# Strassen's block products in part of the first layer's up projection, and new matmul costs in the planner

## The chip, the cores and the metric

The kernel runs on one core of a Trainium2 chip. The time is device microseconds (us) of one execution. The profile was taken in one more execution of the same program; the views of its trace show what each engine did and what it waited for. PE multiplies matrices, DVE is the vector engine, ACT the scalar engine, POOL the GpSimd engine, SP issues most of the DMAs.

## The reference

Two layers work on 512 latent tokens and 256 context tokens of width 1024. Each layer has four head groups and then a gated feed-forward part; all numbers are float32. Only the latent tokens are an output, so the second layer's feed-forward part runs on 512 tokens, the first one's on all 768.

```python
D_FF = 2816
def conv_ffn(h, w_up, conv_w, w_down):
    up = h @ w_up
    a, b = up[..., :D_FF], up[..., D_FF:]
    return (jax.nn.silu(dwconv3(a, conv_w)) * b) @ w_down
...
def trunk_layer(x, xc, c, c_ctx, ang_r, ang_c, layer_idx, ctx_out,
...
    sh1, sc1, gt1, sh2, sc2, gt2 = [m[:, None, :] for m in adaln_params(c, w_ada, b_ada)]
...
    x = x + gt1 * (mix @ w_out)
    x = x + gt2 * conv_ffn(modulate(rmsnorm(x, g2), sh2, sc2), w_up, ffn_conv, w_down)
```

## The kernel before

Everything is kept transposed: features on the 128 partitions, tokens along the free dimension. A float32 product is made of three matmuls of a faster type: each operand is split into a high and a low part, and `passes` (L670) multiplies high by high, high by low and low by high. So every weight tile of 128x1024 (`wr`, one DMA of 512 KB) is cast by ACT (`wh`) and its rest subtracted by DVE or POOL (`wl`); this is `split_units` (L536), and `load_units` (L522) keeps the DMAs of a fixed list, `plan`, ahead of it.

The up projection of one layer has 44 output tiles: 22 feature tiles, each with a half a and a half b. One tile of the first layer is 8 blocks of the contraction x 3 passes x 2 groups of tokens (512 and 256): 48 matmuls (`proj_t`, L677). `up_a` (L1380) takes a tile of a from PSUM through the depthwise convolution (`conv3`: one ACT and four DVE instructions) and the silu; `up_b` (L1387) multiplies by b and splits the product, the hidden tile, into `hi` and `lo`.

The down projection goes by chunks of feature tiles, `FFN_CHUNKS` (L30), in both layers: after the up tiles of a chunk come the down products of the chunk before it, eight output tiles of 128x768. `add_parked` (L1320) scales each from PSUM by ACT (`ev`), and a DMA issued by POOL adds it to `xacc` in DRAM (`dma_add`, L191). The last chunk's products go with `x`, loaded back from `xacc`, into the next norm (`final_pass`, L1280).

While the first layer's feed-forward part runs, `next_ada` (L1351) computes modulation columns, 8 blocks for the first layer and 48 for the second, on DVE: for each a DMA of 512 KB into `adaw`, and one or two products of 1024 elements with a sum along them. It has the lowest priority of all strands. Its buffers take the place of five extra tiles of `S` (`NX`), which the second layer gets when it is done.

No instruction's place is written by hand. `Sched` (L76) is a planner that runs when the program is built: strands (generators) ask for instructions, each with a cost in us (`mms`, L207, for matmuls), and the strand whose instruction could start first gets its place; by the same times an instruction that several engines can do gets its engine. Each engine then runs its instructions in that order. Tiles in SBUF come from `Slots` (L324), 42 of 128x768 (`S`), 3 for raw weights (`WR`) and 5 for each part of a split (`WHI`, `WLO`); PSUM's eight banks come from `Banks` (L367).

## Time and profile before

| | us |
|---|---|
| median of 3 runs | 1537.25 (1537.16 to 1537.35) |
| the profiled execution: time | 1539.82 |
| the profiled execution: span, first to last instruction | 1537.9 |
| PE busy in the span | 1488.2 |
| DVE, ACT, POOL busy in the span | 912.2, 611.9, 246.3 |
| the first layer's feed-forward part, first up matmul to the end of its last products | about 356 to 901 |
| the second layer's attention and its projections | about 940 to 1134 |

The profiled execution took 2.57 us longer than the median, and its time is 1.9 us over its span. A matmul's end is modelled in the trace and matmuls overlap, so a matmul's length says less than the distance from one start to the next, or the count in a window.

### The profile page before, as it was taken

To read this page: it belongs to the slowest core of one execution; us is meant where nothing else is said; L and a number is where in the kernel's file an instruction comes from. 1 tells how busy PE (TensorE), PEld (TensorE's weight loads), DVE (VectorE), ACT (ScalarE), POOL (GpSimd) and SP (SyncE) were. 2 spreads that over 40 slices of the span, in tenths; PEclk is the share of its full clock that TensorE was granted. 3 is DMA by queue.
4 is the path that set the end of the run, shared out by engine and by line. 5 is a ranking of instruction groups with operands and counts; after the bars stand their busy time and mean duration, and the time that the engine had idled before them with its cause. 6 is when DMAs were issued, how large, how long until landed. Compare 5 with 4: busy or idle time off the path is not lost.

```text
span 1537.9 us, 22293 instructions
## 1 busy us (share of the span) xinstructions
PE 1488.2 (97%) x8880; PEld 1259.5 (82%) x8880; DVE 912.2 (59%) x1475; ACT 611.9 (40%) x921; POOL 246.3 (16%) x263
## 2 busy tenths in 40 slices
PE   6999999999999999999999999989989999999997
PEld 4887777887888888888888879867779888888887
DVE  4757888657774746535445277778876443434335
ACT  4445455224333232332322343645534433333332
POOL 0201412013001010010100233144131011010111
PEclk9999999999999999999999999999999999999998
DMA  9573713114437384483763834242322456273644
GB/s 375 167 219 124 218 44 116 59 49 149 164 125 191 123 196 147 140 203 131 178 169 113 181 121 151 88 118 86 111 87 96 125 143 144 96 159 98 143 101 129
DMA packets 70184, 214.36 MB, mean 139 GB/s; under 512 B 9888, under 2 KB 12064, under 8 KB 69952
## 3 DMA queue, kind: packets, MB, share of 16 engines
q1 hardware_dynamic: 49920, 160.39, 32.2%
q0 software_dynamic: 18720, 51.10, 16.0%
q8 instruction: 70, 1.15, 0.3%
q10 hardware_dynamic: 1440, 1.44, 0.3%
q14 instruction: 34, 0.28, 0.1%
HBM read 165.70 MB, written 35.65 MB: 131 GB/s over the span
## 4 chain that ended last, share of the span: by engine, by line
PE 83%; DVE 6%; issue 6%; DMA 4%; ACT 1%; POOL 1%; SPq 0%; DVEq 0%; ACTq 0%; POOLq 0%
PE banks L211 81%; PE banks L224 2%; DVE ss L263 2%; DMA adaw<-in_w_ada 2%; DMA stk<-rlo 1%; POOL xacc L193 1%; DVE p L277 1%; DVE x L277 0%; DVE mx L303 0%; DMA x<-xacc 0%; DVE out L277 0%; DVE hlo L277 0%; DMA mats<-in_mats 0%; SPq L184 0%; ACT wh L253 0%
## 5 line engine op out<-in xcount | busy, mean ns | idle before, releaser
L211 PE MATMUL banks<-hhi,wh 128*128 128x512 f32 (+1 forms) x1392 | 427.6, 358 | 2.6 <-ACT hhi L243 2.4
L211 PE MATMUL banks<-hlo,wh 128*128 128x512 f32 (+1 forms) x1392 | 421.8, 353 | 0.8 <-DVE hlo L277 0.8
L211 PE MATMUL banks<-hhi,wl 128*128 128x512 f32 (+1 forms) x1392 | 420.3, 352 | 0.0
L263 DVE TENSOR_TENSOR wl<-wr,wh 128x1024 fp32r<-128x1024 f32 (+1 forms) x155 | 191.2, 1237 | 177.8 <-ACT wh L253 175.8
L211 PEld LDWEIGHTS banks<-hhi,wh 128*128 128x128 f32 x1392 | 233.8, 190 | 48.2 <-issue 10.2
L211 PEld LDWEIGHTS banks<-hhi,wl 128*128 128x128 f32 x1392 | 234.1, 190 | 38.9
L211 PEld LDWEIGHTS banks<-hlo,wh 128*128 128x128 f32 x1392 | 234.6, 190 | 36.8 <-DVE hlo L277 1.6
L253 ACT CAST wh<-wr 128x1024 fp32r<-128x1024 f32 (+1 forms) x188 | 195.8, 1044 | 149.0 <-PE banks L211 144.2
L193 POOL DMA_DIRECT2D xacc<-ev x80 | 69.2, 865 | 783.7 <-ACT ev L290 710.2
L211 PE MATMUL banks<-hi,wh 128*128 128x512 f32 (+1 forms) x560 | 170.5, 346 | 0.9 <-DVE x L277 0.9
L211 PE MATMUL banks<-lo,wh 128*128 128x512 f32 (+1 forms) x560 | 170.1, 346 | 0.0
L211 PE MATMUL banks<-hi,wl 128*128 128x512 f32 (+1 forms) x560 | 169.5, 344 | 0.0
L277 DVE SCALAR_TENSOR_TENSOR fy<-banks,vec,fy 128x511 f32<-128x511 f32 (+1 forms) x132 | 86.1, 659 | 133.3 <-ACT fy L243 131.4
L290 ACT ACTIVATE ev<-banks,ada 128x512 f32<-128x512 f32 x120 | 69.6, 614 | 148.6 <-PE banks L211 148.4
L265 POOL TENSOR_TENSOR wl<-wr,wh 128x1024 fp32r<-128x1024 f32 (+1 forms) x33 | 80.1, 2428 | 278.8 <-ACT wh L253 247.4
L243 ACT ACTIVATE fy<-banks,vec 128x768 f32<-128x768 f32 (+1 forms) x44 | 34.9, 795 | 215.0 <-PE banks L211 215.0
L211 PEld LDWEIGHTS banks<-hi,wh 128*128 128x128 f32 x560 | 95.0, 188 | 15.3 <-DVE x L277 1.3
L211 PEld LDWEIGHTS banks<-hi,wl 128*128 128x128 f32 x560 | 95.4, 188 | 14.5
L211 PEld LDWEIGHTS banks<-lo,wh 128*128 128x128 f32 x560 | 95.5, 188 | 13.3
L263 DVE TENSOR_TENSOR fy<-banks,fy 128x768 f32<-128x768 f32 (+1 forms) x44 | 36.3, 824 | 92.5 <-PE banks L211 92.4
L277 DVE SCALAR_TENSOR_TENSOR adaw<-adaw,silu 128x1024 f32<-128x1024 f32 x56 | 68.4, 1222 | 28.7 <-DMA adaw<-in_w_adaT 27.8
L303 DVE TENSOR_REDUCE mx<-banks 128x1 f32<-128x768 f32 (+1 forms) x80 | 67.8, 847 | 20.2 <-PE banks L211 19.2
(184 smaller groups left out, 2025.1 us busy)
## 6 DMA issues: line engine op xcount, KB each, us to landing
wr<-in_w_up SPq DMA_DIRECT2D x88, 512.0 KB, 3.7
adaw<-in_w_adaT SPq DMA_DIRECT2D x56, 512.0 KB, 4.5
wr<-in_w_dn SPq DMA_DIRECT2D x44, 512.0 KB, 3.4
adaw<-in_w_ada SPq DMA_DIRECT2D x40, 384.0 KB, 6.1
xacc<-ev POOLq DMA_DIRECT2D x40, 384.0 KB, 6.3
wr<-in_w_zt SPq DMA_DIRECT2D x24, 512.0 KB, 4.5
xacc<-ev POOLq DMA_DIRECT2D x40, 256.0 KB, 4.8
wr<-in_w_o SPq DMA_DIRECT2D x16, 512.0 KB, 3.3
```

The lines of the kernel that those rows point to most:

```text
L193: yield from self.op([("pool", 1.05, lambda: self.nc.gpsimd.dma_start(out, in_, accum_op=ALU.add))], [], [in_])
L211: self.nc.tensor.matmul(o, l, r, start=a, stop=b)
L224: self.nc.tensor.transpose(o, i, ident)
L243: return ("act", cost, lambda: self.nc.scalar.activation(out, in_, func, **k), func), outs, ins
L253: opts.append(("act", 0.19 + n / 1200, lambda: self.nc.scalar.copy(out, in_)))
L263: opts.append(("dve", 0.09 + n / 960, lambda: self.nc.vector.tensor_tensor(out, a, b, op=op)))
L265: opts.append(("pool", 0.1 + n * 2.25e-3, lambda: self.nc.gpsimd.tensor_tensor(out, a, b, op=op)))
L277: lambda: self.nc.vector.scalar_tensor_tensor(out, a, s, b, op0=op0, op1=op1, **k))], outs, ins)
L290: emit = dict(act=lambda: self.nc.scalar.activation(out, a, AF.Copy, scale=s), dve=lambda: self.nc.vector.tensor_scalar(out, a, s, None, o ...
L303: lambda: self.nc.vector.tensor_reduce(out, in_, axis=AX.X, op=op), [out], [in_])
```

## The change

The first layer's up projection has 4 plain feature tiles, as before, and 18 in nine pairs by Strassen's scheme in Winograd's form. A pair has a "quad" for a and one for b. A quad cuts the product of 256 features x 1024 inputs x 768 tokens into 2 x 2 x 2 blocks and makes seven block products in place of eight, each of 4 blocks of the contraction x 3 passes on 384 columns: 84 matmuls in place of 96. The operands' sums are made ahead: those of the weights in `split_quad`, by DVE on the raw tiles, so a quad has 3.5 tiles of 1024 to split where two plain tiles have 2; those of the input once, in `right_factors`. The products' sums are made from PSUM (`half_sums`, `quad_a`, `quad_c`), in four banks of which three are used twice: the products p2, p3 and p4 add to a bank that an engine has read before.

The chunks of the down projection become pairs in both layers (nine of 2 and one of 4, in place of 2, 4, 4, 4, 4, 4), so there are nine additions to `xacc` for each output tile in place of five: 64 more DMAs. There are 44 tiles in `S` and 4 for raw weights; the ring for the descriptors of POOL's DMAs is smaller. The planner takes 0.000449 us for a column of a matmul and 0.004 us with it, in place of 1/2400 and 0.003, and a lower least cost, 0.06.

```diff
-FFN_CHUNKS = [2, 4, 4, 4, 4, 4]
+FFN_CHUNKS = [2] * 9 + [4]
...
-NS = 42
+NS = 44
...
         for o, l, r, a, b in items:
-            c = max(0.107, self.n(r) / 2400 + 0.003)
+            c = max(0.06, self.n(r) * 0.000449 + 0.004)
...
+                for i in range(0, nf, 2):
+                    if quads(l, f):
+                        for c, o in (("a", 0), ("b", 1)):
+                            plan.append((f"q{c}{l}.{f}", [a["w_up"][l, 2 * f + o], a["w_up"][l, 2 * f + 2 + o]], 1024))
+                        f += 2
+                        continue
...
+        def split_quad(key):
...
+            yield from K.when(lambda: len(raws) >= 2)
+            r0, r1 = raws.pop(0), raws.pop(0)
+            rs = yield from WR.get("wr")
+            yield from part(0, r0[:, 0:1024], 1024)
+            yield from K.tt(rs[:, 0:512], r1[:, 0:512], r1[:, 512:1024], ALU.add)
+            yield from K.tt(rs[:, 512:1024], rs[:, 0:512], r0[:, 0:512], ALU.add)
+            yield from part(1, rs[:, 0:1024], 1024)
+            yield from K.tt(r1[:, 0:512], r0[:, 0:512], r1[:, 0:512], ALU.add)
+            yield from part(2, r1[:, 0:1024], 1024)
+            WR.put(r1)
+            yield from K.tt(r0[:, 512:1024], rs[:, 512:1024], r0[:, 512:1024], ALU.add)
+            WR.put(rs)
+            yield from part(3, r0[:, 512:1024], 512)
+            WR.put(r0)
...
                     yield from ada_blocks(0, range(40, 48), 2, AR, silu)
+                    yield from K.when(lambda: "free" in quad_t)
                     yield from ada_blocks(1, range(16), 2, AR, silu)
                     yield from make_a(1, 0)
...
+            def right_factors():
...
+                for q in range(4):
+                    (hi1, lo1), (hi2, lo2) = h2[2 * q], h2[2 * q + 1]
+                    yield from K.when(lambda: all((2 * q + i, g[0]) in h2.done for i in range(2) for g in halves))
+                    b1 = yield from S.get("b1")
+                    yield from K.tt(b1[:, 0:T], hi1[:, 0:T], lo1[:, 0:T], ALU.add, ("pool",))
+                    b2 = yield from S.get("b2")
+                    yield from K.tt(b2[:, 0:T], hi2[:, 0:T], lo2[:, 0:T], ALU.add, ("pool",))
+                    t13 = yield from S.get("t13")
+                    yield from K.tt(t13[:, 0:H], b1[:, 0:H], b1[:, H:T], ALU.subtract)
+                    yield from K.tt(t13[:, H:T], b1[:, H:T], b2[:, H:T], ALU.subtract)
+                    S.put(b1)
+                    t24 = yield from S.get("t24")
...
+                    quad_t[q] = (t13, th, tl, t3)
+                yield from K.when(lambda: state.get("plain") == l)
+                for q in range(4):
+                    t13, th, tl, t3 = quad_t[q]
+                    (hi1, lo1), (hi2, lo2) = h2[2 * q], h2[2 * q + 1]
+                    yield from K.split(hi1[:, H:T], lo1[:, H:T], t13[:, 0:H])
...
+            def product(bank, w, off, b, first):
+                for q in range(4):
+                    yield from K.when(lambda: q in quad_b)
+                    yield from K.mms([(bank[:, 0:H], wp[:, off + 128 * q:off + 128 * q + 128], bp, first and q == 0 and i == 0,
+                                       q == 3 and i == 2) for i, (wp, bp) in enumerate(passes(w, quad_b[q][b]))], not first)
...
+            def quad(key, post):
...
+                K.spawn(post(bk, at), 1)
+                g0 = yield from unit(key + ".0")
+                yield from prod("x", g0, 0, "b11", "p1", True)
+                g1 = yield from unit(key + ".1")
+                yield from prod("y", g1, 512, "t2", "p6", True)
+                yield from prod("z", g1, 0, "t1", "p5", True)
+                unit_done(g1)
+                g2 = yield from unit(key + ".2")
+                yield from prod("w", g2, 0, "t3", "p7", True)
+                yield from K.when(lambda: "x read" in at)
+                yield from prod("x", g0, 512, "b21", "p2", False)
+                unit_done(g0)
+                g3 = yield from unit(key + ".3")
+                yield from K.when(lambda: "z read" in at)
+                yield from prod("z", g3, 0, "b22", "p3", False)
+                S.put(*g3)
+                yield from K.when(lambda: "w read" in at)
+                yield from prod("w", g2, 512, "t4", "p4", False)
+                unit_done(g2)
...
+            def half_sums(bk, at, c22):
...
+                u = yield from S.get("u")
+                yield from K.when(lambda: "p1" in at)
+                yield from K.copy(u[:, 0:H], bk["x"][:, 0:H], ("act",))
+                at.add("x read")
+                yield from K.when(lambda: "p6" in at)
+                yield from K.tt(u[:, H:T], bk["y"][:, 0:H], u[:, 0:H], ALU.add)
+                P.put(bk["y"])
+                yield from K.when(lambda: "p5" in at)
+                yield from K.tt(u[:, 0:H], bk["z"][:, 0:H], u[:, H:T], ALU.add)
+                at.add("z read")
+                yield from K.when(lambda: "p7" in at)
+                yield from K.tt(c22, bk["w"][:, 0:H], u[:, 0:H], ALU.subtract)
+                at.add("w read")
+                return u
...
+            def quad_a(f):
+                def post(bk, at):
...
+                    yield from K.tt(a1[:, H:T], bk["z"][:, 0:H], u[:, H:T], ALU.add)
+                    P.put(bk["z"])
+                    K.spawn(gate(a1, f), 1)
+                    yield from K.when(lambda: "p4" in at)
+                    yield from K.tt(a2[:, 0:H], bk["w"][:, 0:H], u[:, H:T], ALU.subtract)
+                    P.put(bk["w"])
+                    S.put(u)
+                    K.spawn(gate(a2, f + 1), 1)
...
+            def quad_c(f):
+                def post(bk, at):
...
+                    yield from K.when(lambda: "p2" in at and f in ysf)
+                    y = ysf.pop(f)
+                    yield from K.tt(y[:, 0:H], bk["x"][:, 0:H], y[:, 0:H], ALU.mult)
+                    P.put(bk["x"])
...
+                for i in range(0, nf, 2):
+                    if quads(l, f):
+                        state["plain"] = l
+                        yield from quad(f"qa{l}.{f}", quad_a(f))
+                        yield from quad(f"qb{l}.{f}", quad_c(f))
+                        f += 2
...
+QUADS = (0,)
+PLAIN = (4, 4)
...
-NWR = 3
+NWR = 4
...
-    nc = _bacc.Bacc("TRN2", target_bir_lowering=False, num_devices=1)
+    nc = _bacc.Bacc("TRN2", target_bir_lowering=False, num_devices=1, dynamic_dma_scratch_size=4096)
```

On PE, in the first layer's up projection, these rows stand before the change: all three passes of one block of the contraction, each on 512 and on 256 tokens (`hhi` and `hlo` are the input's two parts).

```order
L211 MATMUL banks<-hhi,wh 128x512
L211 MATMUL banks<-hhi,wh 128x256
L211 MATMUL banks<-hlo,wh 128x512
L211 MATMUL banks<-hlo,wh 128x256
L211 MATMUL banks<-hhi,wl 128x512
L211 MATMUL banks<-hhi,wl 128x256
```

With the change these stand there in a quad, the end of the first block product and the start of the second (`th` and `tl` are the two parts of a sum of the input's blocks).

```order
L216 MATMUL banks<-hhi,wh 128x384
L216 MATMUL banks<-hlo,wh 128x384
L216 MATMUL banks<-hhi,wl 128x384
L216 MATMUL banks<-th,wh 128x384
L216 MATMUL banks<-tl,wh 128x384
L216 MATMUL banks<-th,wl 128x384
```

Each row is one matmul: two lengths have become one, and an operand comes from a sum.

On DVE, in the middle of the first layer's feed-forward part, these rows stand before: the convolution of one tile (`fy`), the product with b, and between them the rests of weight tiles (`wl`) and a modulation block (`junk`, `adaw`, `ada`).

```order
L277 SCALAR_TENSOR_TENSOR fy<-banks,vec,fy 128x511 x2
L263 TENSOR_TENSOR wl<-wr,wh 128x1024
L277 SCALAR_TENSOR_TENSOR fy<-banks,vec,fy 128x255 x2
L277 SCALAR_TENSOR_TENSOR junk,ada_92<-adaw,silu 128x1024
L277 SCALAR_TENSOR_TENSOR adaw,ada_92<-adaw,silu 128x1024
L263 TENSOR_TENSOR ada_92<-ada_92,vec 128x2
L263 TENSOR_TENSOR fy<-banks,fy 128x768
L263 TENSOR_TENSOR wl<-wr,wh 128x1024
L263 TENSOR_TENSOR lo<-fy,hi 128x768
```

With the change, at the step from the third pair's quad of a to its quad of b: the last sum of a (`a`, read from PSUM), two convolutions, then the sums that free the banks of b's quad (`u`, `c`).

```order
L268 TENSOR_TENSOR a_5302<-banks,u 128x384
L282 SCALAR_TENSOR_TENSOR fy<-a_5378,vec,fy 128x511 x2
L282 SCALAR_TENSOR_TENSOR fy<-a_5378,vec,fy 128x255 x2
L282 SCALAR_TENSOR_TENSOR fy<-a_5302,vec,fy 128x511 x2
L282 SCALAR_TENSOR_TENSOR fy<-a_5302,vec,fy 128x255 x2
L268 TENSOR_TENSOR u<-banks,u 128x384
L282 SCALAR_TENSOR_TENSOR junk,ada_92<-adaw,silu 128x1024
L268 TENSOR_TENSOR wl<-wr,wh 128x1024
L268 TENSOR_TENSOR u<-banks,u 128x384
L268 TENSOR_TENSOR wl<-wr,wh 128x1024
L268 TENSOR_TENSOR c_5431<-banks,u 128x384
```

The reads of PSUM by which a bank comes free now stand behind convolutions, weight rests and a modulation block.

On DVE, in the second layer's attention, before: the largest score (`mx`), its negative (`nm`), the sums' reciprocal (`s`, `c`), a copy of transposed weights (`aT`).

```order
L303 TENSOR_REDUCE mx<-banks 128x1
L284 TENSOR_SCALAR nm<-mx 128x1
L299 RECIPROCAL s<-s 128x2
L263 TENSOR_TENSOR c<-s,neglam_98 128x1
L256 COPY aT<-banks 128x768
L303 TENSOR_REDUCE mx<-banks 128x1
```

With the change, in the same stretch:

```order
L308 TENSOR_REDUCE mx<-banks 128x1
L289 TENSOR_SCALAR nm<-mx 128x1
L304 RECIPROCAL s<-s 128x2
L268 TENSOR_TENSOR c<-s,neglam_98 128x1
L282 SCALAR_TENSOR_TENSOR adaw,ada_92<-adaw,silu 128x1024
L268 TENSOR_TENSOR ada_92<-ada_92,vec 128x1
L282 SCALAR_TENSOR_TENSOR p<-p,c 128x768
```

A modulation block (`adaw` and `ada`) stands among the attention's instructions. 19 of the 56 blocks now stand there, and 4 in the final pass and the norm ahead of it; before, all stood in the first layer's feed-forward part.

## Rows read from the trace of the kernel before

**Rows 1.** The page of the kernel before: the span and each engine over it

```profile
span 1537.9 us, 22293 instructions
...
PE 1488.2 (97%) x8880; PEld 1259.5 (82%) x8880; DVE 912.2 (59%) x1475; ACT 611.9 (40%) x921; POOL 246.3 (16%) x263
```

**Rows 2.** Windows: us, busy us (count) of PE, PEld, DVE, ACT, POOL; PEclk, DMA

```profile
355.00:901.00 546.00, 544.64 (x3101) 476.26 (x3105) 295.15 (x461) 176.98 (x236) 45.67 (x61) 1.00 0.56 156
901.00:940.00 39.00, 35.58 (x200) 29.63 (x201) 30.18 (x51) 20.16 (x34) 16.00 (x15) 0.96 0.35 121
940.00:1134.00 194.00, 185.78 (x1209) 154.94 (x1208) 153.53 (x248) 99.74 (x164) 62.48 (x55) 0.98 0.35 105
```

**Rows 3.** The chain that ended last: start us, length us, what

```profile
356.85 543.68 PE banks L211 x3092
```

**Rows 4.** Windows as in rows 2, two stretches of even work

```profile
400.00:850.00 450.00, 450.00 (x2576) 394.66 (x2575) 245.41 (x385) 137.43 (x178) 28.49 (x33) 1.00 0.56 155
1200.00:1300.00 100.00, 100.00 (x435) 81.33 (x434) 39.56 (x44) 39.91 (x52) 12.13 (x14) 1.00 0.53 130
```

**Rows 5.** Timeline of PE, a run of 256-column matmuls: start us, length us

```profile
372.02 0.28 PE L211 MATMUL banks<-hhi,wh 128*128 128x256 f32 x1
...
379.75 0.28 PE L211 MATMUL banks<-hhi,wl 128*128 128x256 f32 x1
```

**Rows 6.** Groups on DVE, 400 to 890 us: xcount | busy us, mean ns

```profile
L263 DVE TENSOR_TENSOR wl<-wr,wh 128x1024 fp32r<-128x1024 f32 x58 | 70.7, 1220 | 94.7 <-ACT wh L253 94.7
L277 DVE SCALAR_TENSOR_TENSOR adaw<-adaw,silu 128x1024 f32<-128x1024 f32 x55 | 67.2, 1222 | 28.6 <-DMA adaw<-in_w_adaT 27.8
L277 DVE SCALAR_TENSOR_TENSOR fy<-banks,vec,fy 128x511 f32<-128x511 f32 x38 | 28.5, 749 | 52.8 <-ACT fy L243 52.4
L277 DVE SCALAR_TENSOR_TENSOR junk<-adaw,silu 128x1024 f32<-128x1024 f32 x23 | 28.0, 1216 | 0.0
L277 DVE SCALAR_TENSOR_TENSOR fy<-banks,vec,fy 128x255 f32<-128x255 f32 x40 | 19.2, 479 | 0.7
L263 DVE TENSOR_TENSOR fy<-banks,fy 128x768 f32<-128x768 f32 x20 | 19.2, 958 | 50.1 <-PE banks L211 50.1
L263 DVE TENSOR_TENSOR lo<-fy,hi 128x768 fp32r<-128x768 f32 x20 | 19.0, 952 | 0.0
```

**Rows 7.** Groups on DVE over the whole span

```profile
L263 DVE TENSOR_TENSOR fy<-banks,fy 128x512 f32<-128x512 f32 x22 | 15.2, 691 | 42.3 <-PE banks L211 42.3
L263 DVE TENSOR_TENSOR lo<-fy,hi 128x512 fp32r<-128x512 f32 x22 | 15.0, 684 | 0.0
...
L277 DVE DVE_READ_ACCUMULATOR adaw<-adaw,silu 128x1 f32 x56 | 4.6, 82 | 0.0
```

**Rows 8.** Groups on POOL over the whole span

```profile
L265 POOL TENSOR_TENSOR wl<-wr,wh 128x1024 fp32r<-128x1024 f32 x30 | 72.8, 2427 | 255.7 <-ACT wh L253 224.2 <-PE banks L224 30.4 <-DVE ss L263 1.0
```

**Rows 9.** Groups on ACT, 400 to 890 us

```profile
L253 ACT CAST wh<-wr 128x1024 fp32r<-128x1024 f32 x57 | 59.6, 1045 | 50.5 <-PE banks L211 50.5
L290 ACT ACTIVATE ev<-banks,ada 128x512 f32<-128x512 f32 x40 | 27.5, 688 | 92.0 <-PE banks L211 91.8
L290 ACT ACTIVATE ev<-banks,ada 128x256 f32<-128x256 f32 x40 | 18.6, 466 | 0.0
```

**Rows 10.** Groups on POOL, 400 to 890 us

```profile
L193 POOL DMA_DIRECT2D xacc<-ev x40 | 34.6, 864 | 477.4 <-ACT ev L290 406.9 <-DMA wr<-in_w_dn 70.5
```

**Rows 11.** The page, DMA issues: KB each, median us to landing

```profile
xacc<-ev POOLq DMA_DIRECT2D x40, 384.0 KB, 6.3
```

**Rows 12.** Groups on DVE, 940 to 1134 us

```profile
L277 DVE SCALAR_TENSOR_TENSOR p<-p,c 128x768 f32<-128x768 f32 x16 | 21.6, 1348 | 2.6 <-ACT p L290 1.5 <-POOL p L292 1.0
```

**Rows 13.** Tile adaw: duration ns min/median/max, first and last start us

```profile
L184 SPq DMA_DIRECT2D adaw<-in_w_adaT x56: 327/418/619, 387.0 to 837.2; - x56
L277 DVE SCALAR_TENSOR_TENSOR adaw<-adaw,silu x56: 1212/1224/1227, 395.2 to 845.2; 128x1024 f32<-128x1024 f32 x56
```

125 lines of the change are left out of this document (103 added, 22 removed).

## The prediction

> **What bounds the kernel now.** The page's first part comes first: PE is busy in 1488 of 1538 us, DVE in 912 [rows 1]. A busy PE isn't proof that PE is the limit, so I read the windows by stage: in the first layer's feed-forward part PE has no gap worth counting, 544.6 of 546 us, and DVE is busy in 54% of it [rows 2]. The chain of waits says the same: one piece of 543.7 us is PE alone [rows 3]. There, a matmul less is time less, as long as nothing else gets late. DVE is close to its limit elsewhere: 30 of 39 us around the norm at 901 to 940, and 154 of 194 us in the second layer's attention [rows 2].
>
> **What a matmul costs.** From 400 to 850 us, 2576 matmuls start in 450 us, half with 512 columns and half with 256: 0.1747 us each, for 384 columns in the mean [rows 4]. With 512 alone it is 100/435 = 0.2299 us [rows 4], with 256 alone 7.73/65 = 0.1189 us [rows 5]. No row has 384 columns. By the price of a column at 512 it would be 0.1724, at 256 0.1784; I take 0.1747, since the straight line between 256 and 512 gives 0.1744.
>
> The Trainium skill (TensorE: Matmul & The Clock Gate, Back-to-back issue gap) gives N/2.4 + 2.5 ns at full clock, so an estimate of 162.5 ns for 384 columns and 215.8 for 512; the row at 512 shows 229.9, so this trace doesn't agree. By the page's figures the change below would save 35.1 us.
>
> **Matmuls removed.** A quad has 84 where two plain tiles have 96; 18 quads take 1512 in place of 1728. Before: 1728 x 0.1747 = 301.9 us. After: 1512 x 0.1747 = 264.2. Saved: **37.7 us**; with the two other prices, 41.2 and 32.1.
>
> **DVE in a pair.** A pair with its down products is 264 matmuls, 46.1 us of PE (before 288, 50.3). DVE's work in it, from the order of the change and the durations of before [rows 6, 7]: 8 weight rests x 1.220 = 9.8; 8 sums of raw weights at 512, 5.5 (as `lo` at 512, 0.684); 2 rests at 512, 1.4; 12 reads or products at 384, 6.7 (0.558, on the line through 0.691 at 512 and 0.958 at 768); two convolutions, 4 x 0.749 + 4 x 0.479 = 4.9; one product of 768 and two rests, 2.9; two modulation blocks of 2 x (1.22 + 0.08) + 0.16, 5.5. That is 36.7 us, or 39.4 with three blocks: 80 to 85% of PE's time. So DVE keeps up over a pair. The order within it is the risk.
>
> **Where PE can wait.** Bank z must be read before p3, the sixth product: 5 x 12 x 0.1747 = 10.5 us into the quad; bank w before p4, at 12.6. The tight place is the quad of b, shown in the change: when p4 of a's quad ends, DVE has in order the last sum (0.56), two convolutions (4.9), a read (0.56), a modulation product (1.30), a weight rest (1.22) and the read of z (0.56): 9.1 us. Another rest and the read of w end at 10.9. So 1.4 and 1.7 us are left, without the time a semaphore takes. Late by that much costs nothing; more goes to PE one for one, since p3 and p4 and all later products stand behind the waiting matmul. Of nine pairs I expect a third of a microsecond each, **+3**; the bounds are 0 and nine times 1.4, 13. Quads of a follow 16.8 us of down products, and DVE catches up there.
>
> **Sums of the input.** `right_factors` gives DVE 16 sums at 384 elements, 4 rests at 768 and 8 at 384, 17 us, while PE does 4 plain features and a chunk, 84 us. In that stretch DVE has 69 us by its order, and 8 adds on POOL (768 elements, 1.8 us each by 2427 at 1024 [rows 8]) can slow it by a few. It fits. The last four rests come at the first quad's start, before p5 needs them at 4.2 us. Taken **+2**, bounds 0 and 8.
>
> **The doubled additions.** ACT has 8 x (0.688 + 0.466) = 9.2 us in 16.8 us of down products, and 26 of 46 us in a pair with casts at 1.045 [rows 9]; POOL 8 x 0.864 = 6.9 [rows 10]. A tile `ev` is held for 0.69 + 0.47 + 0.86 + 6.3 [rows 9 to 11] = 8.3 us, and outputs come each 2.1 us, so four must be free where two were enough. The slots went from 42 to 44, and the order reuses such a tile after six outputs. Taken 0. With three free it would be 2.8 us an output: 5.3 a pair, 48 in all. In the second layer the same additions stand against 11 us of down products a pair: 8 x 0.688 on ACT, covered. The fourth raw tile and the smaller ring I take at 0; no row shows a wait for either.
>
> **The late modulation blocks.** Before, all 56 stood under the long PE stretch, the last at 845 us [rows 13], where DVE had room. Now DVE is fuller and the second layer's blocks start later. Four blocks of 1.22 + 0.08 + 0.16 = 1.46 us stand in the norm, 5.8 us on a DVE that has 9 us free of 39 and on which PE waits; taken **+3** (0 to 5.8). Nineteen stand in the attention: 27.7 us, so DVE goes from 154 to 181 of 194 us, with PE at 186 [rows 2]. PE has other products to do there, so most is hidden; taken **+5** (0 to 27.7). Until they are done the five extra tiles of the second layer's attention are closed, which is in the same bound.
>
> **New costs in the planner.** They change places everywhere. At most PE's 8.2 idle us in the attention can be won, about as much lost; taken 0.
>
> **Sum.** -37.7 + 3 + 2 + 3 + 5 = -24.7, against the profiled execution's own 1539.8: 1515.1. It ran 2.57 us over the median of the runs, so **1512.5 us**. With these terms near nothing (+3) it is 1503; with 40% of their upper bounds (0.4 x 54.5 = 22) it is 1522.
>
> **Rivals.**
>
> The late blocks decide. If all 23 lie on the path, 33.6 us in place of my 8: -37.7 + 5 + 33.6 = +0.9, 1538; half of it gives 1521. For it: DVE at 93% in the attention, and two-input work there already stretched (`p<-p,c`, 768 elements, 1.348 us [rows 12] against 0.952 [rows 6]). Against: PE is at 96% there and DVE's idle time is spread over the stage. 1522 to 1534: 0.15.
>
> DVE takes the quads. `p<-p,c` shows the price of contention, +42%; on all DVE work of a pair with two SBUF operands, 29.7 us, that is +12.5: 49 us with two blocks, 52 with three. It decides from 46.1 on, that is from +32%; at 50.3 nothing is won. In nine pairs 28 to 52 us are lost, in half of them 14 to 26: 1523 to 1551 with none to all of my other terms. Against: POOL, with which DVE shares, hardly computes in this stage. Chance 0.15.
>
> The Trainium skill (GPSIMD Engine Reference, 1. Specifications) states that GpSimd's SBUF interfaces are shared with VectorE, with contention for DVE instructions with two SBUF inputs. The stretched row agrees, and the feed-forward rows, where POOL only issues DMAs, show none.
>
> The additions decide, the way to a slower kernel: if fewer than four `ev` tiles are free in a down stretch, ACT waits for landings, banks stay full and PE stops: 48 us with three, so 1512.5 + 48 = 1560. For it: some 40 of 44 tiles are held then: 16 of `h2`, 12 of its sums, 8 hidden, 4 of weights. Against: the distance of six in the order. 0.06.
>
> The 384-column matmul costs as much as 512: 1512 x 0.2299 = 347.6, 45.7 slower than before, 1596 with my other terms. The row at 256 speaks against it, since there a weight load fits in 0.119 us. 0.02.
>
> No stall at all and the cheap price: 1537.25 - 41.2 = 1496; 1496 to 1503: 0.05.
>
> **Chances.** The forecast keeps 0.57. Within 0.2% (1534.2 to 1540.3) is what a measurement here can't tell from no change. Faster: 0.57 + 0.15 + 0.05 + 0.06 of DVE's rival = 0.83; same: 0.04 of it; slower: its 0.05, the additions and the dear matmul, 0.13. The range 1501 to 1533 leaves out 0.03 below and 0.17 above; the likeliest case's own is 1503 to 1522.
>
> **What the profile will show.** Right if the matmuls of 384 columns start 0.172 to 0.178 us apart; if the first layer's feed-forward part is 30 us or more shorter and PE idles in it for less than 10 us, named after DVE `u`, `a` or `c`; if DVE is at 75 to 88% there; and if the attention from the second norm to the last `wo` products is longer by 3 to 10 us with `adaw` rows in it. Wrong if PE waits for `ev` or for `wl`, if the landing of the additions rises well over 6.3 us, if the granted clock falls in the quads, or if the attention grows by more than 15 us.

## The result and the profile after

The changed kernel takes 1545.85 us (median of 5 runs, 1544.7 to 1551.43), the kernel before 1537.25 on the same chip: ratio 1.0066, 95% interval 1.0046 to 1.0087. It is slower by 0.7%, where 1512.5 was forecast. The profiled execution has 1545.21 us.

The page and windows of the changed kernel (columns as in [rows 2]; the last four answer to [rows 2, 4]):

```profile
span 1543.4 us, 22548 instructions
...
PE 1465.2 (95%) x8664; PEld 1264.6 (82%) x8664; DVE 1041.9 (68%) x1697; ACT 710.1 (46%) x1086; POOL 351.1 (23%) x352
```

```profile
355.00:901.00 546.00, 527.35 (x2986) 492.03 (x2985) 423.25 (x635) 263.89 (x388) 115.90 (x116) 0.99 0.60 163
...
470.00:800.00 330.00, 330.00 (x1887) 315.07 (x1886) 253.90 (x384) 170.14 (x252) 59.23 (x64) 1.00 0.66 170
901.00:940.00 39.00, 33.47 (x165) 27.08 (x164) 32.26 (x61) 17.02 (x27) 11.18 (x14) 0.89 0.44 156
940.00:1134.00 194.00, 177.98 (x1093) 145.19 (x1093) 162.04 (x277) 97.33 (x157) 61.11 (x51) 0.96 0.46 148
1200.00:1300.00 100.00, 100.00 (x433) 81.05 (x433) 38.22 (x43) 45.21 (x60) 20.87 (x24) 1.00 0.69 162
```

The quads themselves run as forecast: from 470 to 800 us PE has no gap, with DVE at 77%. A stretch of one quad and the start of the next holds 384 columns alone: the 88th matmul starts 15.26 us after the first, 0.1754 us apart.

```profile
602.67:617.93 15.26, 15.26 (x88) 15.03 (x87) 10.65 (x15) 5.98 (x9) 2.75 (x3) 1.00 1.06 273
```

So 216 matmuls are gone at about the price taken, and the time came back elsewhere. Five stages, cut in the timeline at the starts of PE's last product with `mhi,wl` in each layer (the end of its attention) and its last product with `hi,wl` (the end of its down projection), tell where:

| stage, us | before | after | difference |
|---|---|---|---|
| start to the end of the first attention | 349.3 | 356.8 | +7.5 |
| first layer's feed-forward part | 561.8 | 545.8 | -16.0 |
| second layer's norm and attention | 238.9 | 252.3 | +13.4 |
| second layer's feed-forward part | 375.9 | 377.8 | +1.9 |
| tail | 12.0 | 10.7 | -1.2 |

Below, PE's "loss" in a stretch is the time between starts of consecutive matmuls above 0.2299, 0.1750 and 0.1187 us for 512, 384 and 256 columns (0.45 ns a column otherwise), where it is over 0.03 us; it holds idle time and a lower clock. In and around the feed-forward part it grew at three places: from 350 to 400 us 5.8 before and 11.9 after (1.7 of it is the end of the first attention, which lies ahead of 350 in the kernel before), from 440 to 470 none and 12.5, at the final pass (890 to 920) 6.2 and 13.4.

The middle one in the chain of waits of the changed kernel:

```profile
439.68 1.16 DVE junk L282 x2
...
440.86 7.98 DMA adaw<-in_w_adaT
...
448.86 1.24 DVE junk L282 x2
...
450.12 1.25 DVE adaw L282 x2
...
451.73 0.69 ACT ev L295
...
452.46 3.39 PE banks L216 x10
...
468.29 3.78 PE banks L216 x20
```

and in its waits, ACT's from 420 to 500 us and PE's from 435 to 470:

```profile
ACT ev L295 <- DVE ada L268: 10.1, 3, 4.2
...
ACT ev L295 <- DMA xacc<-ev: 2.2, 1, 2.2
```

```profile
PE banks L216 <- ACT ev L295: 7.4, 2, 4.8
PE banks L216 <- DVE u L268: 0.7, 1, 0.7
```

A modulation block waits for its DMA, a down product's scaling (`ev`) waits for that block, and PE for the bank. The blocks are the eight of the first layer's gate, and an output tile needs the column of its own block alone. Before, the first down product started at 456.0 us, and the eighth column, ready at 455.0, was first used at 473.0:

```profile
454.80 0.16 DVE L263 TENSOR_TENSOR ada<-ada,vec 128x2 f32<-128x2 f32 x1
```

```profile
472.96 0.69 ACT L290 ACTIVATE ev<-banks,ada 128x512 f32<-128x512 f32 x1 [1.04 <-PE banks L211]
```

It had 18 us to spare, and the other seven had more. Now both sides have moved. The first down product starts at 435.0, 21 us earlier, and the columns are ready 30 to 43 us later: the first at 429.5 in place of 396.6, the eighth, whose block ends at 492, at 498.1. The first block's DMA is issued at 361.3 us, but DVE begins its first product only at 412.0, behind the sums of the input and the rests of weight tiles. From 390 to 430 us DVE is busy in 38.1 us of 40, where it was in 29.5 (before, then after, columns as in [rows 2]):

```profile
390.00:430.00 40.00, 40.00 (x231) 35.11 (x230) 29.52 (x46) 11.78 (x13) 0.00 (x0) 1.00 0.46 156
```

```profile
390.00:430.00 40.00, 39.67 (x235) 34.89 (x234) 38.09 (x56) 22.99 (x28) 6.23 (x3) 1.00 0.17 53
```

```profile
412.00 1.65 DVE L282 SCALAR_TENSOR_TENSOR junk<-adaw,silu 128x1024 f32<-128x1024 f32 x1
```

The granted clock is at half (1.2 GHz) there for 3.4 and 6.8 us, after PE's gaps of 2.6 and 4.8 us. At half, 384 columns start 0.32 us apart, so that some 4 of the 12.5 us are the clock's. A window in it:

```profile
459.00:465.60 6.60, 4.66 (x15) 4.66 (x16) 3.46 (x7) 1.46 (x3) 0.85 (x1) 0.50 0.54 121
```

### The profile page after: what moved, and what is told of

It is laid out like the page before. It is cut to its first block, busy times and chain, and to the rows that moved or that the text cites. A ratio compares the mean times of both kernels' runs of the same rounds, so it can differ in the third digit from the quotient of the medians.

```text
span 1543.4 us, 22548 instructions
## 1 busy us (share of the span) xinstructions
PE 1465.2 (95%) x8664; PEld 1264.6 (82%) x8664; DVE 1041.9 (68%) x1697; ACT 710.1 (46%) x1086; POOL 351.1 (23%) x352
## 4 chain that ended last, share of the span: by engine, by line
PE 72%; DVE 16%; DMA 5%; issue 4%; ACT 2%; SPq 1%; POOL 1%; DVEq 0%; ACTq 0%; POOLq 0%
PE banks L216 70%; DVE mx L308 2%; DVE hlo L282 2%; DVE wl L268 1%; DVE ss L268 1%; DVE adaw L282 1%; DMA adaw<-in_w_adaT 1%; PE banks L229 1%; DVE ht L282 1%; SPq L189 1%; DMA stk<-rlo 1%; DMA stk<-rhi 1%; DVE p L282 1%; DMA wr<-in_w_zt 1%; DVE x L282 1%
## 5 line engine op out<-in xcount | busy, mean ns | idle before, releaser
L216 PE MATMUL banks<-hhi,wh 128*128 128x512 f32 (+2 forms) x1032 | 355.5, 367 | 9.5 <-ACT ev L295 4.8
L216 PE MATMUL banks<-hlo,wh 128*128 128x512 f32 (+2 forms) x1032 | 348.0, 360 | 7.0 <-DVE hlo L282 7.0
L216 PE MATMUL banks<-hhi,wl 128*128 128x512 f32 (+2 forms) x1032 | 346.9, 359 | 0.0
L268 DVE TENSOR_TENSOR wl<-wr,wh 128x1024 fp32r<-128x1024 f32 x173 | 213.7, 1239 | 131.9 <-ACT wh L258 120.6
L258 ACT CAST wh<-wr 128x1024 fp32r<-128x1024 f32 x206 | 214.9, 1045 | 167.9 <-PE banks L216 124.2
L198 POOL DMA_DIRECT2D xacc<-ev x144 | 124.8, 867 | 523.3 <-ACT ev L295 521.1
L295 ACT ACTIVATE ev<-banks,ada 128x512 f32<-128x512 f32 x216 | 124.6, 615 | 83.4 <-PE banks L216 64.0
L216 PEld LDWEIGHTS banks<-hi,wl 128*128 128x128 f32 x560 | 96.3, 190 | 14.4
L248 ACT ACTIVATE p<-banks,nm 128x768 f32<-128x768 f32 x64 | 57.6, 900 | 67.6 <-DVE nm L289 31.9
L282 DVE SCALAR_TENSOR_TENSOR x<-banks,ada,x 128x256 f32<-128x256 f32 (+1 forms) x88 | 49.1, 574 | 42.9 <-PE banks L216 23.5
L216 PE MATMUL banks<-wh,hhi 128*128 128x256 f32 x256 | 75.2, 294 | 0.7 <-DVE au L261 0.7
```

Of the source, the lines that this page charges most:

```text
L198: yield from self.op([("pool", 1.05, lambda: self.nc.gpsimd.dma_start(out, in_, accum_op=ALU.add))], [], [in_])
L216: self.nc.tensor.matmul(o, l, r, start=a, stop=b, skip_group_check=more)
L248: return ("act", cost, lambda: self.nc.scalar.activation(out, in_, func, **k), func), outs, ins
L258: opts.append(("act", 0.19 + n / 1200, lambda: self.nc.scalar.copy(out, in_)))
L268: opts.append(("dve", 0.09 + n / 960, lambda: self.nc.vector.tensor_tensor(out, a, b, op=op)))
L282: lambda: self.nc.vector.scalar_tensor_tensor(out, a, s, b, op0=op0, op1=op1, **k))], outs, ins)
```

## The experiments

**Theory.** The products were saved, but (1) the down products come before their gate columns, since the first one stands after 4 plain tiles in place of 6, (2) the short last stretch no longer covers the additions and the loads of `x`, (3) the late modulation blocks cost time in the second attention, (4) the planner's new costs lose time in the first attention. **Rivals:** DVE's load in the first quad makes the middle loss; slow landings (10.0 us in place of 6.3 [rows 11]) make it; any new order moves the attention by as much. Ratios are to the kernel before on the same chip, with 95% intervals.

### The new costs alone, in the kernel before

```diff
-            c = max(0.107, self.n(r) / 2400 + 0.003)
+            c = max(0.06, self.n(r) * 0.000449 + 0.004)
```

> The kernel before, with the new matmul costs in the planner alone. In the changed kernel the last output product (operand mhi,wl) of the first layer's attention starts at 356.75 us, before at 349.27, and neither Strassen nor the chunks stand ahead of it. Theory (the loss there is the planner's costs, placing matmuls longer): this product starts at 355 to 358 us, and the kernel is 4 to 10 us slower than before, 1541 to 1547. Rival (the place of the costs is neutral, the shift comes from elsewhere, a worse fit of the weights' DMAs): start at 348 to 351 us and 1535 to 1540.

1550.8 us, 1.0077 (1.0047 to 1.0108): more than expected. The first attention ends at 356.1, 6.9 later than before; the rest is spread, 2.8 us in the first feed-forward part, 3.0 in the second attention, 2.7 in the second feed-forward part, and the tail is 1.6 shorter.

### The old costs in the changed kernel

The same edit back.

> The changed kernel with the old matmul costs in the planner. Theory (planner's costs lose 7.5 us in the first attention): the last output product there starts at 349 to 351 us, and the kernel is 5 to 9 us shorter than the changed one, 1537 to 1541, if the later stages keep their gaps. Rival (the new costs help in the quads, where 384 columns at the old price would let the planner think PE slower or faster than it is): the first attention wins 7 us, and the feed-forward part and the second attention lose it again, 1544 to 1552.

1557.6 us, 1.0130 (1.0107 to 1.0153). The first attention ends at 353.7, 3.0 earlier; the second one takes 263.8 us, 11.5 more than in the changed kernel. The rival holds in kind, and the time is even above its range: the costs can't be judged by one stage.

### The gate blocks at the highest priority

```diff
                     yield from ada_blocks(0, range(40, 48), 2, AR, silu)
+                    K.spawn(ada_rest(cm, AR, silu), 5)
+                def ada_rest(cm, AR, silu):
                     yield from K.when(lambda: "free" in quad_t)
...
-                K.spawn(next_ada(), 5)
+                K.spawn(next_ada(), 0)
```

> The changed kernel with the eight modulation blocks of the first layer's gate at the highest priority; the second layer's 48 stay at the lowest. In the changed kernel the last of the eight ends at 468 us and PE loses some 12.5 us between 440 and 470, where ACT waits for a gate column before it can scale the first down products. Theory (the gate columns are late, because the first chunk of down products now comes after 4 feature tiles in place of 6): the loss from 440 to 470 falls under 3 us, and the kernel is 8 to 13 us shorter, 1533 to 1538. Rival (the late second-quad reads and weight rests on a full DVE make this loss): the gap stays, named after wl or u, and the time stays within 1542 to 1549.

1550.3 us, 1.0077 (1.0056 to 1.0099). It didn't do what it meant: the eighth block ends at 479.5 (492 in the changed kernel; the 468 of the expectation is when the sixth column is ready), since each still waits for one of two tiles and a DMA, and the loss only moved, to 410 to 490. It doesn't test the theory.

### The sums on POOL later

```diff
             def right_factors():
+                yield from K.when(lambda: state.get("mid"))
```

> The changed kernel with the eight sums of the input on POOL begun only when all of the norm's instructions have their places. In the changed kernel hlo of 512 columns takes 2.1 to 2.2 us on DVE where POOL's b runs beside it, 0.75 elsewhere, and PE loses 11.9 us from 350 to 400 us where it lost 5.8 before. Theory (POOL's sums stretch DVE's two-input work in the norm): hlo there falls to 0.75 us, the loss from 350 to 400 to 5 to 7 us, and the kernel is 3 to 7 us shorter, 1539 to 1543. Rival (the norm isn't on the path at that point, since the loss is won back while PE waits for the gate columns at 440 to 470): hlo falls but the time stays within 1544 to 1548.

1547.5 us, 1.0055 (1.0037 to 1.0073). The planner gave the same instructions in the same order on every engine as in the changed kernel, since the sums wait for `hlo` by their data anyway: no test, but a second measurement of the changed kernel. It agrees within the intervals; its profiled execution has 548.3 and 255.2 us for the feed-forward part and the second attention, where the first had 545.8 and 252.3, so 3 us in a stage are within the spread.

### The first chunk of four

```diff
-FFN_CHUNKS = [2] * 9 + [4]
+FFN_CHUNKS = [4] + [2] * 7 + [4]
```

> The changed kernel with the down projection's chunks as 4, seven of 2, and 4, in both layers: the first down product comes after the 4 plain feature tiles and the first pair in place of 4 feature tiles, and there are 8 additions for each output tile in place of 9. In the changed kernel the first down product starts at 435 us, but the eighth gate block ends at 492 (before: 456 and 454.8), and PE loses 12.5 us from 440 to 470. The run with the gate blocks at the highest priority doesn't test this, since there the eighth still ends at 480 and the first down product starts at 441. Theory (gate columns late for the earlier down products): first down product at 460 to 475, PE's loss between 430 and 500 under 4 us, the feed-forward part from first up product to last down product 532 to 538 us in place of 545.7, and the kernel 8 to 13 us shorter than the changed one, 1533 to 1538. Rival (DVE's load in the first quad makes the loss): the loss from 440 to 500 stays at 9 or more, and 1543 to 1550.

1540.6 us, 1.0014 (0.9999 to 1.0028). The first down product starts at 471.8, PE waits for no `ev`, and the feed-forward part takes 537.7 (545.8). The gate blocks come no earlier there (the eighth ends at 497.6), so moving the products back is enough to end this wait. A loss of 6.2 of the 12.5 stays at the first quad, named after `u` and `hlo`, and the time lies between the two forecasts: theory and the first rival share the place.

### Without the gate blocks

```diff
+                if l == 0:
+                    which = 2
...
-                    yield from K.when(lambda: (l, 40 + j) in done_ada)
-                    yield from K.scale(y[:, c], p[:, c], gt(l, 5, j, v), EVQ)
+                    yield from K.when(lambda: (l, (40 if l else 16) + j) in done_ada)
+                    yield from K.scale(y[:, c], p[:, c], gt(l, 5 if l else 2, j, v), EVQ)
...
-                    yield from ada_blocks(0, range(40, 48), 2, AR, silu)
```

> The changed kernel without the first layer's eight gate blocks (16 products of 1024 and 8 DMAs left out): the down products are scaled by the columns of the other gate, which are there long before, so that neither the wait nor this work is left. Theory (gate columns late): PE's loss between 430 and 500 falls from 12.5 to under 3 us, and the kernel is 9 to 15 us shorter than the changed one, 1531 to 1537, more if the second layer's blocks come earlier by it. Rival (slots: ev tiles wait for their additions' landing, 10.0 us here where it was 6.3): ACT still waits for landings in the first down products and PE's loss there stays over 6 us.

1534.9 us, 0.9984 (0.9969 to 0.9999). The loss from 440 to 470 falls from 12.5 to 1.1 and the feed-forward part to 533.7, 12.1 less. Of PE's waits from 430 to 500 us this is left:

```profile
PE banks L216 <- ACT ev L295: 0.6, 1, 0.6
```

The additions still land as late (10.1 us), and ACT waits 6.6 us for them while PE loses 1.1: the slots' rival falls. The run leaves out DVE's work too, so the 12 us are the wait and that work together.

### Without the last 22 modulation blocks

```diff
-                    yield from ada_blocks(1, range(16, 48), 1, AR, silu)
+                    yield from ada_blocks(1, range(16, 26), 1, AR, silu)
+                    for j in range(26, 48):
+                        yield from K.tt(ada[1][:, j:j + 1, 0:1], bias(1, j, 1)[:, :, 0:1], bias(1, j, 1)[:, :, 0:1], ALU.add)
+                        done_ada.add((1, j))
```

> The changed kernel without the second layer's last 22 modulation blocks (their columns are twice the bias; 22 products of 1024 and 22 DMAs left out), which are those that stand in the second norm and attention there. Theory (the late blocks lose time on a full DVE and keep the five extra tiles closed): from the last down product of the first layer to the last output product of the second layer's attention it takes 252.3 us in the changed kernel and 238.9 before; without them 238 to 243, and the kernel is 9 to 14 us shorter, 1532 to 1537. Rival (the order that the new costs give loses it): 249 to 254 us stay, and 1543 to 1548.

1538.6 us, 1.0007 (0.9994 to 1.0021). The norm and attention take 243.9 us (252.3): 8.4 of the 13.4 are these blocks. The loss at the final pass stays (15.2), so that isn't theirs. The attention's window, against 162.04 us of DVE and 177.98 of PE above:

```profile
940.00:1134.00 194.00, 183.84 (x1171) 151.58 (x1169) 148.47 (x242) 101.06 (x164) 55.83 (x53) 0.97 0.34 101
```

### The chunks alone, in the kernel before

```diff
-FFN_CHUNKS = [2, 4, 4, 4, 4, 4]
+FFN_CHUNKS = [2] * 9 + [4]
```

> The kernel before, with the chunks of the down projection as nine of 2 and one of 4 and nothing else: 64 more additions, the first down products after 4 feature tiles in place of 6. Theory (gate columns late): the first down product starts at 422 to 428 us, ahead of the eighth gate block at 455; PE waits for ACT ev, 8 to 25 us, and the kernel is 8 to 25 us slower than before, 1545 to 1562. Rival one (the wait is made by the quads, not by the chunks): 1536 to 1541. Rival two (the additions' landing is what costs, all along the feed-forward parts): slower, with waits for xacc landings spread over 430 to 900 us and 1160 to 1530.

1547.9 us, 1.0070 (1.0048 to 1.0091), slower as expected, but elsewhere. The first down product starts at 423.3, 39 us ahead of the eighth block's end, and PE loses nothing from 420 to 470. So the earlier products alone cost nothing there: the eighth block ends at 462.4, close to the 454.8 of before, ACT waits 4.2 us for columns, and PE goes on with other tiles. The wait of the changed kernel needs the rest of the change too. Its later columns fit that, and so does that a plain tile takes 2 of 8 banks and a quad 4; the two weren't tried apart. The loss is at the final pass, 16.7 us from 900 to 930 in place of 7.4, and 5 blocks came late, after the last down product's start.

### Short stretches only at the end, and only at the start

The kernel before with 7 chunks each:

```diff
-FFN_CHUNKS = [2, 4, 4, 4, 4, 4]
+FFN_CHUNKS = [2, 4, 4, 4, 2, 2, 4]
```

> The kernel before with the chunks 2, 4, 4, 4, 2, 2, 4: the down stretch ahead of the final pass has 2 feature tiles in place of 4, in both layers; the first down product and the gate blocks stay where they were; 7 additions for each output tile where it has 5 with its six chunks. Theory (the short stretch no longer covers the additions' landing and the loads of x): DVE waits 5 us or more for x<-xacc, PE loses 13 to 17 us from 880 to 930 in place of 7, and 1541 to 1546. Rival (nine additions, or a mere change of order, made the loss with all chunks short): PE's loss there stays at 7 to 9 us, and 1535 to 1540.

```diff
-FFN_CHUNKS = [2, 4, 4, 4, 4, 4]
+FFN_CHUNKS = [2, 2, 2, 4, 4, 4, 4]
```

> The control: the kernel before with the chunks 2, 2, 2, 4, 4, 4, 4, as many additions as the run before it, but the short stretches at the start, so that the first down product comes at about 423 us, ahead of the eighth gate block, and the stretch ahead of the final pass is as it was. Theory: no more than 2 us of PE's time at the gate columns, since plain tiles follow there and leave banks free, the norm as before, 1535 to 1540. Rival (more additions cost by themselves, or the early gate columns do): 1541 to 1547.

1540.9 us, 1.0030 (1.0018 to 1.0043), and 1536.8, 1.0000 (0.9986 to 1.0015). PE's loss from 900 to 930 is 11.8 and 7.5 (before 7.4). DVE's wait for `x`, from 850 to 935 us, before, with the short end and with the short start:

```profile
DVE x L277 <- DMA x<-xacc: 0.8, 1, 0.8
```

```profile
DVE x L277 <- DMA x<-xacc: 7.5, 3, 3.4
```

```profile
DVE x L277 <- DMA x<-xacc: 3.2, 3, 1.9
```

The short stretch ahead of the final pass costs 4 us; wait and place are the theory's, but loss and time fall short of its ranges. As many additions elsewhere cost nothing.

### The loads of x on SP

With the first chunk of four:

```diff
-                yield from K.dma(t[:, 0:T], xacc[l][j][:, 0:T], ("pool",))
+                yield from K.dma(t[:, 0:T], xacc[l][j][:, 0:T], ("sp",))
```

> As the run with the chunks 4, seven of 2, 4 (1540.6 us), with the eight loads of x from xacc ahead of the final pass issued by SP in place of POOL. There and in the changed kernel DVE waits some 8 us for x<-xacc in the last down products, and PE loses 13 to 15 us from 880 to 920; the kernel before with the chunks alone does the same. Theory (the last down stretch lasts 16.8 us in place of 33.5 and no longer covers the additions' landing of 10 us and the load of 6.5; on POOL a load that waits for a landing also holds back the additions behind it): DVE's wait for x<-xacc falls to 2 to 5 us, PE's loss there to 8 to 11, and 1534 to 1538. Rival (the landing of the last addition alone sets it, whatever queue loads): the wait stays at 7 to 9 us and the time at 1539 to 1543.

1554.0 us, 1.0114 (1.0097 to 1.0132), 13 us worse. DVE's wait for `x` falls from 8.5 to 5.3 and the loss from 880 to 920 from 14.7 to 12.0, as the theory has it, but the second attention takes 262.3 us in place of 254.2, with the same 20 blocks in it (those that start more than 20 us after the last down product); PE waits there 6.7 us for ACT `p`, which it didn't before. Why the order fell out so stays open.

### The old costs up to the second norm

On top of it; and, with the loads of `x` on POOL again, the second:

```diff
+        self.late = False
...
-            c = max(0.06, self.n(r) * 0.000449 + 0.004)
+            c = (max(0.06, self.n(r) * 0.000449 + 0.004) if self.late else max(0.107, self.n(r) / 2400 + 0.003))
...
-                    state["mid"] = True
+                    state["mid"] = K.late = True
```

> As the run before it, with the old matmul costs in the planner up to the first layer's second norm and the new ones from there on. Theory (the new costs lose time in the first attention): the last output product there starts at 350 to 354 us in place of 356 to 358, and the kernel is 3 to 6 us shorter than the run before it. Rival (what the first part wins the later order loses, as with the old costs throughout): no gain, within 2 us, or longer.

> The changed kernel with the chunks 4, seven of 2, 4, and the old matmul costs in the planner up to the first layer's second norm; the loads of x stay on POOL. Theory (the two priced parts add up): the last output product of the first attention at 350 to 352 us, the feed-forward part at 537 to 540, and 1532 to 1536. Rival (the second attention's length depends on the order by 8 us either way): it takes over 258 us, and 1538 to 1546.

1547.6 us, 1.0071 (1.0056 to 1.0086): the first attention ends at 351.4, and 6.4 us are won, as expected. On POOL 1535.7 us, 0.9992 (0.9978 to 1.0006), as fast as the kernel before and no faster: the first attention ended at 355.5 in its profiled execution, though every engine has the same order up to there as in the run at 351.4. One execution's end of that stage has such a spread; over runs with the same order there it is 350.9 to 355.5, mean 353.0 (seven runs, old costs in the changed kernel), 355.8 to 358.9, mean 357.0 (eight, new costs), 349.0 to 350.9, mean 349.5 (four, the kernel before and its chunk variants). So the costs are 4.0 of the 7.5 us and the other 3.5 come with the rest of the change (slots, raw tiles), untested apart.

### The modulation blocks among the quads

The first with `x` on SP, the third as the kernel of 1535.7 us; the second is the first with the old costs up to the second norm:

```diff
                     yield from ada_blocks(0, range(40, 48), 2, AR, silu)
+                    K.spawn(ada_rest(cm, AR, silu), 1)
+                def ada_rest(cm, AR, silu):
                     yield from K.when(lambda: "free" in quad_t)
...
```

> As the first of these runs, with the second layer's 48 modulation blocks at the priority of the quads' strands in place of the lowest: by the order 49 of the 56 blocks then stand ahead of the last quad's reads and none in the second attention, where 16 to 17 stood. Theory (late blocks lose 8 us in the attention, and DVE has room for them in the quads, at some 41 of 46 us a pair): PE keeps its even pace in the quads, the attention takes 241 to 246 us in place of 254, and the kernel is 6 to 10 us shorter than the first of these. Rival (DVE is then too full in the quads, and PE waits for u, a, c or wl there): PE idles 6 us or more between 470 and 830, and the gain is under 3 us or a loss.

> The last three edits together. Theory (they lose time at different places and add up): 1522 to 1530 us, faster than the kernel before. Rival (each new order of the planner moves the attention by some us either way, so that gains don't add up): 1531 to 1541.

```diff
-                    K.spawn(ada_rest(cm, AR, silu), 1)
+                    K.spawn(ada_rest(cm, AR, silu), 1.5)
```

> The kernel of 1535.7 us (chunks 4, seven of 2, 4; old costs up to the second norm) with the second layer's modulation blocks at a priority between the quads' strands and the weights' splits: by the order 8 blocks stand in the second attention in place of 17, and 8 more among the quads. Theory (DVE has some room in the quads, at 77% there, so that half of the blocks fit): the way from the last down product to the last output product falls from 252 to 245 to 249 us, the feed-forward part grows by less than 3, and 1529 to 1533, faster than both kernels. Rival (ahead of the weights' splits each block delays a rest of weights, and PE waits for wh or wl): the feed-forward part grows by 5 us or more, and 1534 to 1541.

1553.8 us, 1.0116 (1.0097 to 1.0135); 1549.3, 1.0084 (1.0067 to 1.0101); 1537.9, 1.0001 (0.9991 to 1.0011). In the first the attention falls from 262.3 to 241.3 us, and the feed-forward part grows from 540.7 to 559.9. The rival holds, at the place that the prediction named, the step from a quad to the next; the second, 1549.3, is above both of its ranges. The first one's chain of waits:

```profile
568.50 0.75 DVE fy L282
569.25 1.15 DVE junk L282 x2
...
570.43 1.24 DVE adaw L282 x2
...
571.77 0.57 DVE u L268
...
572.43 0.56 DVE u L268
...
574.75 1.04 ACT wh L258
...
575.81 1.24 DVE wl L268
...
577.09 2.95 PE banks L216 x9
```

A block of two products stands behind the convolutions and ahead of the reads (`u`) that free the banks, and the weights come after them. With half of the blocks there (the third) 1.7 us are won in the attention and 3.7 lost in the feed-forward part. A fourth division sent 16 of the one-product blocks ahead alone:

```diff
-                    yield from ada_blocks(1, range(16, 48), 1, AR, silu)
+                    K.spawn(ada_single(cm, AR, silu, 32), 1)
+                def ada_single(cm, AR, silu, n):
+                    yield from ada_blocks(1, range(16, n), 1, AR, silu)
+                    K.spawn(ada_end(cm, AR, silu, n), 5)
...
```

> The same kernel of 1535.7 us with 16 of the second layer's one-product blocks at the priority of the quads' strands, after the 16 of two products: by the order 34 of the 56 blocks stand ahead of the last quad's reads in place of 30, 11 in the final pass and the norm, 11 in the attention in place of 17. Theory: 3 to 4 us off the attention, nothing lost in the quads, 1531 to 1534. Rival (they now stand in the final pass and the norm, where PE waits for DVE already): PE's loss from 880 to 920 grows by what the attention wins, and 1534 to 1538.

1541.7 us, 1.0020 (1.0009 to 1.0031). The attention takes 260.2 us with 16 late blocks, longer than 251.9 with 20: neither theory nor rival.

### Two chunks of four at the end

The kernel of 1535.7 us with

```diff
-FFN_CHUNKS = [4] + [2] * 7 + [4]
+FFN_CHUNKS = [4] + [2] * 5 + [4] + [4]
```

> As the run before it, with the chunks 4, five of 2, 4, 4: the down stretch ahead of the final pass has its 4 feature tiles back, and by the order all 56 modulation blocks stand ahead of the last quad's reads. Theory (short last stretch and late blocks were the rest of the loss): PE's loss from 880 to 930 is 6 to 9 us, the second layer's way from the last down product to the last output product 239 to 246 us in place of 252, and 1515 to 1526, faster than the kernel before. Rival (16 hidden tiles beside the 28 of the input and its sums leave no tile for the quads' sums, so that the last quads wait for tiles and the planner puts the blocks into that wait): PE idles over 10 us between 600 and 880, and 1530 to 1550.

1605.5 us, 1.0455 (1.0430 to 1.0479): the rival in kind, though far above its range. With all blocks done early the norm and attention take 238.2 us, but one wait in the last quads takes 65. PE's and ACT's, 800 to 890 us:

```profile
PE banks L217 <- ACT s4h L259: 64.8, 1, 64.8
```

```profile
ACT fy L249 <- DVE adaw L283: 70.4, 1, 70.4
```

ACT's `fy` starts when the last modulation block is done, which is when the kernel turns the blocks' buffers into the five extra tiles.

## Why the prediction was wrong

**The matmul price** was right: 0.1754 us where 0.1747 was taken. By the formula that the Trainium skill (TensorE: Matmul & The Clock Gate, Back-to-back issue gap) gives for an isolated matmul it would be 0.1625; the window doesn't agree.

**The second quads' reads** (+3): nothing from 470 to 800. The tight place is real, as the blocks among the quads show, but with the blocks at the lowest priority it isn't reached. The rival that DVE takes the quads didn't come either: `wl` is 1.221 us there, as in [rows 6]. The +42% that it was priced by is a mean: the 16 instructions behind the 1.348 us of [rows 12] took 1.00 to 2.56 us, with a median of 1.01.

**The sums of the input** (+2): about right as a price. In the 50 us behind the end of the first attention the loss is 5.8 before, 10.1 after, 8.9 with the new costs alone and 8.8 with the old costs in the changed kernel: 1 to 3 us are left for the sums. But "it fits" didn't ask what stands behind them on DVE. The gate blocks do, and they came 30 us and more later.

**The doubled additions** (0) is the step that failed first. It asked only whether `ev` tiles come back in time, and there it was nearly right (2.2 us of ACT's wait, landings at 10.0). It didn't ask what the shorter chunks move. They bring the first down product 21 us forward, ahead of gate columns that the fuller DVE had meanwhile put back by 30 to 43 us (12 us by the run without the gate blocks, 8 by the first chunk of four). They also halve the stretch that covers the loads of `x` (4 us in the kernel before, where that alone was changed). That the gate columns needed both, the earlier products and the rest of the change, is shown by the chunks alone, which lost nothing there; that the rest is DVE's load is read from the trace and not tested apart. [Rows 13] held half of the warning: the first of 56 blocks starts its last product at 395.2 us and one comes each 8.2, so the eighth ends at about 454. With the first down product at 435 the eighth tile is scaled some 17 us later, at 452: 2 us too early for its column even if no block is delayed.

**The late modulation blocks** (+3 and +5): the sum agrees with the 8.4 us of the run without them, but by luck. Without them the loss at the final pass stays, so that the +3 in the norm isn't theirs; the attention from 20 us behind the last down product loses 41.3 us in place of 51.1, so that 9.8 are theirs where 5 was taken. No cheaper place was found: among the quads they cost as much or more.

**The planner's costs** (0, within 8) is the second step that failed: on the kernel before they cost 12 us, 7 to 17 by the interval, of which 6.9 are in the first attention, a stage that the change doesn't touch otherwise than by its slots and raw tiles. There PE's loss of 62 us in 349 shows a stage with many waits, which leave more to lose than the 8 us that the prediction took from the second attention. (There too the loss before is 47 us, not the 8 us of idle time.) In the changed kernel their price is smaller: the old costs throughout are some 10 us slower, and up to the second norm alone they win 3 to 6.

**The sum**, by profiled executions: -37.7 for the matmuls; +12 gate columns; +3 sums; +4 short last stretch; +8 late blocks; +7.5 first attention; +0.7 second feed-forward part and tail: -2.5. The measured difference is +5.5. Where the 8 us between lie can be read from the loss. It grew by 4.3 in the 50 us behind the first attention, by 14.4 from there to 30 us before the last down product, by 6.1 from there to 20 us after it, and by 10.0 in the rest of the second attention, against the 3, 12, 4 and 8 of the sum. With -37.1 for the matmuls by the same prices, +7.5 and +0.7 this makes +5.9, so no place is missing. The causes of these 8 us are not settled: the new costs alone bring 3 us at the first place, the other prices were measured in other orders, and one execution's stages spread by 3 us and more; of the second attention the runs with the same 20 late blocks have 252 to 264 us. No rival of the prediction came as it stood. What made the kernel slower is the sum of several losses, of which the largest, the gate columns, stood in none of them.

**The signs** that the prediction set: the matmuls and DVE's share came as forecast, but the feed-forward part is 16 us shorter and not 30. Three of its signs of being wrong showed: PE waits for `ev`, additions land after 10.0 us, and the granted clock falls in the first quad.

## What to carry to other kernels

When a change cuts the work of a stage that is full, list what the old length of its parts covered: a producer of low priority that finished in time, a landing, a load. The margin is read from the trace, for each use by itself, as the end of its producer against the use (455.0 and 473.0 here for the eighth column). Ask of both ends how the change moves them: here the use came 21 us forward and the producer, behind a fuller engine, 43 us back; the first alone cost nothing. Where a planner orders the instructions, time a change of its costs by itself before anything else is added: here it lost 12 us on a kernel with the same work.

## What the runs showed of the hardware

The additions to DRAM land later with the change: 10.0 us in the median for 384 KB where [rows 11] have 6.3, in the page of the changed kernel:

```profile
xacc<-ev POOLq DMA_DIRECT2D x72, 384.0 KB, 10.0
...
xacc<-ev POOLq DMA_DIRECT2D x72, 256.0 KB, 7.1
```

Their number is a part of it: the kernel before has 7.1 and 7.4 with 48 of them, and with as many as the changed kernel:

```profile
xacc<-ev POOLq DMA_DIRECT2D x72, 384.0 KB, 8.2
```

What makes the other 1.8 us stays open.

A product of two SBUF operands on DVE took up to three times as long while POOL computed: `hlo` of 512 columns 2.20 us beside POOL's `b`, 0.75 alone. The Trainium skill (GPSIMD Engine Reference, 1. Specifications) states that contention; the size is from these rows of DVE's timeline:

```profile
371.39 0.48 DVE L282 SCALAR_TENSOR_TENSOR hlo<-ht,ada,hhi 128x256 fp32r<-128x256 f32 x1
371.79 0.48 DVE L282 SCALAR_TENSOR_TENSOR ht<-x,acol,rstd 128x256 f32<-128x256 f32 x1
372.33 2.20 DVE L282 SCALAR_TENSOR_TENSOR hlo<-ht,ada,hhi 128x512 fp32r<-128x512 f32 x1
```
